# Expert stage of a two-block transformer layer: GpSimd's arithmetic given to VectorE and ScalarE, the gate matrix spread over 72 up tiles, the gather moved later

## The chip, the cores and the metric

One NeuronCore of a Trainium2 chip runs the whole program in one launch. The metric is device time in microseconds. In this text PE is TensorE, DVE is VectorE, ACT is ScalarE, POOL is GpSimd and SP is SyncE, which only issues DMAs here. Each engine works through its own list of instructions in order, so an instruction that waits holds back all that stand behind it on its engine.

## The reference

512 tokens of width 1024 pass two transformer blocks in float32. The first block has stick-breaking attention, a state-space branch, cross-attention and a feed-forward network. The second has window attention, gated linear attention and, at its end, the part that the change touches: a feed-forward network of 16384 product-key experts.

```
q = (h @ wq).reshape(B, S, PEER_HEADS, 2, PEER_QDIM // 2)
sub_scores = jnp.einsum('bshpk,hpnk->bshpn', q, subkeys)
top_v, top_i = lax.top_k(sub_scores, PEER_TOPK)
...
best_v, best_pos = lax.top_k(cand, PEER_TOPK)
gates = jax.nn.softmax(best_v, axis=-1)
...
ub = jnp.take(u, eb, axis=0)
hid = gelu(jnp.einsum('tkd,td->tk', ub, xb)) * gb
return jnp.einsum('tk,tkd->td', hid, jnp.take(v, eb, axis=0))
```

Each token chooses 128 experts (8 heads times 16). An expert has a first and a second key number, both below 128. Its row of `u` gives a hidden value, which is weighted by its gate and multiplied with its row of `v`.

## The kernel before

**Tiling.** The tokens form four tiles of 128. For the first three tiles (384 tokens) the kernel multiplies with all experts on PE and sets the gates of the experts that a token hasn't chosen to zero. The 16384 experts are 128 expert tiles. An "up tile" is u h for one of them: 24 matmuls of 128x384 (L126 to L128: 8 slices of the width, each as three products of high and low parts). A "down tile" adds its part of the output: 18 matmuls of 128x512. The last token tile gathers instead: 128 rows of `u` and 128 rows of `v` for each token, each step one indirect DMA (L1272) of 128 rows, then one DVE instruction, a dot product (L1282) or an accumulation (L74).

**Split of a weight.** A weight tile `ws` of 128x1024 arrives by an SP DMA (L106). ACT writes its high part (L77, `wh` or `hi`), then L118 subtracts it to get the low part (`wl` or `lo`). `lo_pool` sends the subtraction to POOL, otherwise it is DVE's. Before the change POOL subtracts for half of the last 12 query weights (L1142) and for all but the first of the 128 up tiles (L1302, L1411); the down weights are DVE's.

**Gates and gate matrix.** `gates` turns the top-16 lists of a token tile into key numbers and gates (`sel`), nearly all of it on DVE. `matrix` then makes, for each of the 128 tokens of a tile, a 128x128 matrix of gates over (first key, second key): `o1` is the one-hot of the 128 first keys, `o2` the one-hot of the second keys times the gate (L1234, DVE), and their product on PE (L1235; the profile counts two PE instructions for each). The work goes by groups of 4 tokens, 32 groups for a tile, 96 in all. `MIX` says who makes a group's `o1`: DVE in one instruction (D, L1229), POOL in four (P, L1232), or ACT in five (A, L1227 and L1228: four of |key - column|, one of max(0, 1 - that)). ACT copies each group's product to `G` (L1236), and every 8 groups an ACT DMA takes `G` to DRAM (`scr_g`, L1238).

**Three parts of the stage.** In the up part, `NST` up tiles run while `select` makes the gates and the matrix, `SS` steps of it for each tile; their hidden values go to DRAM (`scr_h`). From tile `EA` on, `RA` gather steps follow each tile. In the ring the other 128 - NST expert tiles have their up and down tiles in turn, with `GA` gather steps each. In the down-only part the down tiles of the first NST follow, with `GB` gather steps each, and hidden values and gates are read back. In the up part a planner lays out each engine's list from the order of the code and its own costs; from the ring on the order is that of the code (L1389 and after).

Of the kernel before, what the change touches and what calls it, by code (L numbers as in the profile page):

```python
# [15 lines left out]
OP = mybir.AluOpType  # L16
# [13 lines left out]
class Split:  # L30
    """A float32 tensor as two float32r parts whose sum is exact."""
# [8 lines left out]
class Kern:  # L40
# [14 lines left out]
    def big(self, pool):  # L55
        """Split [128, 8, 512] in a pool that holds one of them."""
        return Split(pool.tile([128, 8, 512], F32R, name="hi"), pool.tile([128, 8, 512], F32R, name="lo"))

    def open_norm(self, ctx, bufs=2):
        """Room for the rows and the scratch of the norms over D."""  # L60
        self.rows = ctx.enter_context(self.tc.tile_pool(name="rows", bufs=bufs, reuse_waits="tile"))

# [22 lines left out]
    def row_dma(self, t, src, n, eng=None):  # L85
        """A row of DRAM to all partitions."""
        (eng or self.nc.gpsimd).dma_start(t, bass.AP(tensor=src.tensor, offset=src.offset, ap=[[0, 128], [1, n]]))
# [6 lines left out]
    def split_to(self, dst, src, scale=None):  # L94
        """dst.hi, dst.lo from a float32 source; the scale is applied in float32 first."""
# [34 lines left out]
    def tmode(self, ps, w, hT, m=128, nk=8, first=True, last=True):  # L130
        """ps[m, tok] += (nk k-tiles of w)^T hT."""
# [3 lines left out]
    def staggered(self, ws, hT):  # L135
        """tmode for each of ws, the first half of the tokens first; the pending tiles of hT come between."""
# [8 lines left out]
    def nmode(self, ps, ws, hT, tt, k0=0, first=True, last=True):  # L145
        """ps[tok tile tt, 512] += hT^T (two k-tiles in each w)."""
# [18 lines left out]
    def transpose_split(self, src, dst, tt, k0=0, nk=8):  # L165
        """src [128 tok, nk*128] -> dst[:, k0 + k, tok tile tt]."""
# [14 lines left out]
    def norm_T(self, x, row, dst, tt, shift=None, keep=None, wait=False):  # L181
        """dst's token tile tt = the normed x, transposed; with wait, its last part comes with flush()."""
# [8 lines left out]
    def post_norm(self, pss, row, x):  # L191
        """x += rms_norm(the two banks) * row."""
# [6 lines left out]
    def log1p(self, pool, e, out, shape, tag):  # L199
        """out = log(1 + e) for 0 <= e <= 1, as 2 artanh(e / (2 + e))."""  # L200
# [14 lines left out]
# ======================================================================  # L215
# stick-breaking attention
# ======================================================================
def stick_breaking(K, hT, oT, wv, fill):
    tc, nc, I = K.tc, K.nc, K.I
    with ExitStack() as st:  # L220
# [22 lines left out]
        def project(hp, nm):  # L243
            """Queries or keys of two heads. For head j, q2[:, j] holds the queries' high parts in its own
            half of the partitions and the low parts in the other, k2[:, j] the keys' high parts in both
            and kl the keys' low parts in its own."""
# [17 lines left out]
        def weights(h):  # L264
            """The weights of head h, by query."""
# [25 lines left out]
        def values(h, rows):  # L291
            """The weighted values of head h, in three steps."""
# [48 lines left out]
# ======================================================================  # L341
# state-space branch
# ======================================================================
def ssd_steps(K, hT, p):
    """dt and its decays: dt, the cumulative sums of a dt, their exponentials and dt times the decay to
    the chunk's end, by token; the sums and the decay over a chunk by head in DRAM."""
# [48 lines left out]
def ssd(K, hT, acc, steps, last, merge):  # L395
    scr, nat, cd = steps
    tc, nc, I = K.tc, K.nc, K.I
    with ExitStack() as st:
# [29 lines left out]
        def front(g):  # L428
            """The projections of group g; a piece of them at each step."""
# [113 lines left out]
# ======================================================================  # L543
# first block
# ======================================================================
def nmode_pairs(K, name, nk, hT, pool, done, loads=lambda dh: None):
    """hT^T W for a W of 1024 columns, token tile by token tile; loads(dh) starts after each half of W."""
# [18 lines left out]
def block1_mix(K, hT):  # L566
    """The merged branches, transposed, in the buffer of hT."""
    tc, nc, I = K.tc, K.nc, K.I
    scr = K.dp.tile([8, 128, 2, 512], F32, name="scr_br")
    with ExitStack() as st:  # L570
# [50 lines left out]
        def last():  # L621
            """Gates of the state-space branch, beside its last group."""
# [25 lines left out]
# ======================================================================  # L648
# cross-attention
# ======================================================================  # L650
# [10 lines left out]
def mem_kv(K, mT, kT, v):  # L661
    """Keys (transposed) and values of the memory."""
# [15 lines left out]
def queries(K, p, hT):  # L678
    """The queries of a head, transposed, at each step."""
# [50 lines left out]
# ======================================================================  # L730
# feed-forward network
# ======================================================================
# [54 lines left out]
# ======================================================================  # L787
# second block
# ======================================================================
# [11 lines left out]
def modulation(K):  # L801
    """silu(c) w_ada + b_ada, as a row in DRAM, the scales as 1 + scale times the norm's weights; a tile of
    w_ada at each step."""
# [37 lines left out]
def gla_gates(K, q, hT, b):  # L841
    """b: per-chunk cumulative sums of log a, transposed."""
# [27 lines left out]
def window_attention(K, q, pq, qT, kT, vT, mixT):  # L870
    """Sliding-window attention, a block of queries in three steps."""
# [52 lines left out]
def gla_scores(K, A, lm, zp, b, gq, gk):  # L924
    """A[c][s, head, t]: the decayed products of keys and queries within a chunk, a level of the
    hierarchy of halves at each step."""
# [40 lines left out]
def gla_out(K, pw, pq, A, b, gq, gk, v, sg, mixT):  # L967
    """The states before the chunks, then the outputs of all chunks, gated by sg. The room is that of the
    attention's tiles."""
# [57 lines left out]
def block2_mix(K, p, hT, gv, mixT):  # L1027
    """Attention over a window and gated linear attention, transposed, in mixT, and the first half of the
    output projection of two token tiles."""
    tc, nc, I = K.tc, K.nc, K.I  # L1030
    with ExitStack() as st:
# [9 lines left out]
        with ExitStack() as sw:  # L1041
# [22 lines left out]
            def gates(tt):  # L1064
                """silu(gg) and the norm's weights."""
# [32 lines left out]
# ======================================================================  # L1098
# product-key experts
# ======================================================================  # L1100
# The tokens of the first three tiles meet all experts on the tensor engine, weighted by a matrix of
# gates that is zero where an expert isn't chosen; those of the last tile gather their experts' rows.
# [3 lines left out]
NST = 56  # L1106
SS = 2.4
GA = 2.4
RA = 1.4
EA = 18  # L1110
MIX = "DPDA"
GB = 0.7
# [4 lines left out]
def top16(K, sc, tv, ti):  # L1117
    """The 16 largest values of sc in descending order, and where they are; sc is overwritten."""
# [8 lines left out]
class Peer:  # L1127
# [3 lines left out]
    def queries(self, p):  # L1131
        """The 16 best keys of each half query of each token."""
# [4 lines left out]
        for f in range(16):  # L1137
            if f < 4:
                ps = first[f]
            else:  # L1140
                ps = K.gsum()
                K.tmode(ps, K.weight(I["w_pq"][f], lo_pool=f % 2 > 0), self.hT)  # L1142
# [10 lines left out]
    def gates(self, w, tt):  # L1153
        """sel: for each token of the tile and each of its 128 choices, both key numbers and the gate. Pair
        (a, b) of the sorted keys has (a + 1)(b + 1) - 1 others before it that are no smaller, so the 16 first
        of all 256 are among (0, b), (a, b < 8) for 0 < a < 8 and (a, 0), kept here in the order of the pairs."""
# [50 lines left out]
    def matrix(self, w, tt, sel):  # L1207
        """The gates of a tile's tokens for all experts, to DRAM."""
# [6 lines left out]
        for tb in range(0, 128, TB):  # L1215
            G = K.pA.tile([128, 128, TB], F32, name="G", tag="lo" if tb // TB % 2 else "hi")
            Gt = G.rearrange("p b t -> p t b")
            for t0 in range(0, TB, 4):
# [9 lines left out]
                elif who == "D":  # L1228
# [413 lines left out]
```

## Time and profile before

| | |
|---|---|
| time before, median of 3 runs | 3011.12 us (3010.54 to 3011.23) |
| span of the profiled execution | 3010.5 us |
| PE busy | 2898.0 us, 96% |
| DVE busy | 2127.6 us, 71% |
| ACT busy | 1219.5 us, 41% |
| POOL busy | 1143.6 us, 38% |
| DMA | 536.17 MB, mean 178 GB/s |

The profiled execution has no time of its own beside its span; the span lies 0.6 us below the median of the runs. A busy share over the whole span says little here, since the parts differ: the rows below are cut by part, at the first up matmul (1739), the first one-hot matmul (1810), the end of the last one (2138), the first down matmul (2167) and the last up matmul (2757).

### The profile page before, as it was taken

The numbers are of one execution on the slowest core, as the hardware profiler recorded it, in microseconds if no ns is written. First come the engines' busy times: TensorE is split into PE (matmuls) and PEld (weight loads), VectorE is DVE, ScalarE is ACT, GpSimd is POOL, SyncE is SP. The second block draws the span as 40 slices with busy tenths as digits, with TensorE's granted clock in tenths as the row PEclk, the third lists the DMA queues.
The fourth block names the chain that finished last, engine by engine and source line by source line (L and its number), as shares of the span: only waits on it lengthen the run. The fifth ranks groups of instructions, "written<-read, shape, count | busy, mean of one in ns | idle before, by whom it ended". The sixth has DMA issues, their size and how long they took to land.

```text
span 3010.5 us, 38769 instructions
## 1 busy us (share of the span) xinstructions
PE 2898.0 (96%) x14347; PEld 2419.2 (80%) x14347; DVE 2127.6 (71%) x3449; ACT 1219.5 (41%) x1914; POOL 1143.6 (38%) x824
## 2 busy tenths in 40 slices
PE   8999999999999999999999988878999999999998
PEld 6666777777798877787768888878899999998886
DVE  4776355776665656545776998988788888887875
ACT  4654244333344333123443346666333333333333
POOL 0221253342210100001221255777788878775310
PEclk9999999999999999999999998999999999999999
DMA  4112423233542466432203244777898888889983
GB/s 166 50 38 65 159 74 112 81 90 127 185 137 94 140 225 197 139 124 81 62 29 121 84 155 149 254 243 254 292 316 297 293 302 297 299 299 318 344 298 132
DMA packets 212937, 536.17 MB, mean 178 GB/s; under 512 B 17518, under 2 KB 97822, under 8 KB 211084
## 3 DMA queue, kind: packets, MB, share of 16 engines
q1 hardware_dynamic: 151040, 346.27, 35.0%
q0 software_dynamic: 38560, 139.05, 13.3%
q10 hardware_dynamic: 23148, 48.37, 4.5%
q8 instruction: 113, 1.85, 0.3%
q14 instruction: 76, 0.62, 0.1%
HBM read 491.07 MB, written 42.56 MB: 177 GB/s over the span
## 4 chain that ended last, share of the span: by engine, by line
PE 42%; DVE 9%; issue 1%; ACT 1%; POOL 0%; POOLq 0%; ACTq 0%
PE pg L127 9%; PE pg L126 9%; PE pg L128 9%; PE pa L128 4%; PE pa L127 4%; PE pa L126 4%; DVE o L1234 3%; PE pa L1235 2%; DVE oh L1194 1%; DVE gr L1282 1%; DVE o L1229 1%; PE pa L935 1%; PE pg L919 0%; DVE bits L1192 0%; PE pa L1147 0%
## 5 line engine op out<-in xcount | busy, mean ns | idle before, releaser
L126 PE MATMUL pg<-hi,wh 128*128 128x512 f32 (+3 forms) x2272 | 830.8, 366 | 0.5 <-ACT hi L77 0.5
L127 PE MATMUL pg<-lo,wh 128*128 128x512 f32 (+3 forms) x2272 | 829.7, 365 | 0.0
L128 PE MATMUL pg<-hi,wl 128*128 128x512 f32 (+3 forms) x2272 | 825.0, 363 | 2.6 <-POOL wl L118 2.6
L77 ACT ACTIVATE wh<-ws 128x1024 fp32r<-128x1024 f32 (+1 forms) x454 | 461.3, 1021 | 535.0 <-PE pg L127 321.6
L118 POOL TENSOR_TENSOR wl<-ws,wh 128x1024 fp32r<-128x1024 f32 (+1 forms) x177 | 465.5, 2635 | 339.3 <-ACT wh L77 291.3
L118 DVE TENSOR_TENSOR wl<-ws,wh 128x1024 fp32r<-128x1024 f32 (+1 forms) x277 | 331.8, 1205 | 213.6 <-ACT wh L77 213.0
L126 PEld LDWEIGHTS pg<-hi,wh 128*128 128x128 f32 (+1 forms) x2272 | 430.2, 190 | 54.9 <-issue 4.0
L127 PEld LDWEIGHTS pg<-lo,wh 128*128 128x128 f32 (+1 forms) x2272 | 431.0, 190 | 53.5 <-issue 3.5
L128 PEld LDWEIGHTS pg<-hi,wl 128*128 128x128 f32 (+1 forms) x2272 | 430.3, 189 | 52.9 <-POOL wl L118 3.0
L161 POOL TENSOR_SCALAR ss<-ss 128x1 f32<-128x1 f32 x54 | 15.3, 283 | 621.0 <-ACT junk L77 620.0
L1272 POOL DMA_INDIRECT gr<-in_peer_v,idx x128 | 198.4, 1550 | 123.3 <-DVE acc L74 99.1
L74 DVE SCALAR_TENSOR_TENSOR acc<-gr,hid,acc 128x1024 f32<-128x1024 f32 x127 | 234.7, 1848 | 9.1 <-DMA gr<-in_peer_v,idx 7.2
L1282 DVE SCALAR_TENSOR_TENSOR gr<-gr,h 128x1024 f32<-128x1024 f32 x128 | 225.5, 1791 | 12.7 <-DMA gr<-in_u_rows,idx 12.5
L1272 POOL DMA_INDIRECT gr<-in_u_rows,idx x128 | 189.6, 1481 | 78.7 <-DVE gr L1282 47.0
L77 ACT ACTIVATE hid<-pg 128x384 f32<-128x384 f32 x128 | 62.6, 489 | 303.8 <-PE pg L128 303.6
L126 PE MATMUL pg<-wh,hi 128*128 128x512 f32 x448 | 181.8, 407 | 2.0 <-ACT hi L77 2.0
L1234 DVE TENSOR_SCALAR o<-io,sT 128x128 f32<-128x128 f32 x384 | 164.6, 500 | 26.6 <-PE pa L1235 26.6
L128 PE MATMUL pg<-wh,lo 128*128 128x512 f32 x448 | 179.9, 402 | 3.3 <-DVE lo L98 1.7
L127 PE MATMUL pg<-wl,hi 128*128 128x512 f32 x448 | 179.8, 401 | 3.2 <-POOL wl L118 2.0
L77 ACT ACTIVATE ah<-hid 128x384 fp32r<-128x384 f32 x128 | 67.2, 525 | 260.0 <-DVE hid L68 255.7
L1235 PE MATMUL pa<-o,o 128*128 128x128 f32 x768 | 110.2, 291 | 55.8 <-DVE o L1234 52.0
L1235 PEld LDWEIGHTS pa<-o,o 128*128 128x128 f32 x768 | 102.2, 199 | 62.9 <-issue 28.3
(426 smaller groups left out, 5197.0 us busy)
## 6 DMA issues: line engine op xcount, KB each, us to landing
ws<-in_peer_u SPq DMA_DIRECT2D x128, 512.0 KB
ws<-in_peer_v SPq DMA_DIRECT2D x128, 512.0 KB
ws<-in_w_ada SPq DMA_DIRECT2D x48, 512.0 KB
scr_g<-G ACTq DMA_DIRECT2D x12, 2048.0 KB
gt<-scr_g SPq DMA_DIRECT2D x32, 768.0 KB
ws<-in_w_xbc SPq DMA_DIRECT2D x24, 512.0 KB
ws<-in_w_gate SPq DMA_DIRECT2D x22, 512.0 KB
ws<-in_w_up SPq DMA_DIRECT2D x22, 512.0 KB
```

The lines of the kernel that those rows point to most:

```text
L74: return self.nc.vector.scalar_tensor_tensor(out, a, s, b, op0=op0, op1=op1)
L77: return self.nc.scalar.activation(out, in_, f, **k)
L118: eng.tensor_tensor(w.lo, s, w.hi.bitcast(F32), op=OP.subtract)
L126: mm(ps, a.hi, b.hi, start=first, stop=False)
L127: mm(ps, a.hi, b.lo, start=False, stop=False)
L128: mm(ps, a.lo, b.hi, start=False, stop=last)
L935: nc.tensor.matmul(ps[:, i, :], l[hp, i, ls], r[hp, i, rs], start=True, stop=True)
L1194: nc.vector.copy_predicated(T[:, :, :, :n], bits[:, :, :, None].to_broadcast([128, 8, TOPK, n]), src)
L1234: self.o2_last = nc.vector.tensor_scalar(o2[:, t, :], self.io, sT[:, 1, c:c + 1], sT[:, 2, c:c + 1], op0=OP.is_equal, op1=OP.mult)
L1235: nc.tensor.matmul(pg_[:, t, :], o1[:, t, :], o2[:, t, :], start=True, stop=True)
L1272: nc.gpsimd.indirect_dma_start(out=r, out_offset=None, in_=table, in_offset=bass.IndirectOffsetOnAxis(ap=self.idx[:, z, k:k + 1], axis=0))
L1282: nc.vector.scalar_tensor_tensor(rows[k], rows[k], 1.0, self.h3, op0=OP.mult, op1=OP.mult, accum_out=self.dot[:, k:k + 1])
```

## The change

POOL keeps no arithmetic in the expert stage: `lo_pool` falls away for the query weights and the up tiles, so their subtractions go to DVE, and `MIX` has no P group. Of four groups three now have their `o1` from ACT and one from DVE, where it was one and two. `NST` rises from 56 to 72, with fewer steps of gates and matrix for each tile (`SS` 1.8, was 2.4). The gather takes 0.8 steps for each late up tile (was 1.4), 3.0 for each ring tile (was 2.4) and 0.6 for each down-only tile (was 0.7). Docstrings and comments are dropped as well, which moves line numbers by 3 (L1234, L1272 and L1282 become L1231, L1269 and L1279).

```
-NST = 56
-SS = 2.4
-GA = 2.4
-RA = 1.4
+NST = 72
+SS = 1.8
+GA = 3.0
+RA = 0.8
 EA = 18
-MIX = "DPDA"
-GB = 0.7
+MIX = "AADA"
+GB = 0.6
...
-                K.tmode(ps, K.weight(I["w_pq"][f], lo_pool=f % 2 > 0), self.hT)
+                K.tmode(ps, K.weight(I["w_pq"][f]), self.hT)
...
-                elif who == "D":
+                else:
                     nc.vector.tensor_tensor(o1, self.io[:, None, :].to_broadcast([128, 4, 128]), ...
-                else:
-                    for t, c in enumerate(cs):
-                        nc.gpsimd.tensor_scalar(o1[:, t, :], self.io, sT[:, 0, c:c + 1], None, op0=OP.is_equal)
...
-        w = w or K.weight(K.I["peer_u"][e], lo_pool=e > 0)
+        w = w or K.weight(K.I["peer_u"][e])
...
-                        us[jobs[i]] = K.wsplit(us[jobs[i]], lo_pool=True)
+                        us[jobs[i]] = K.wsplit(us[jobs[i]])
```

The first place is DVE's list where the gates of the last token tile are worked out, before any one-hot (`pos`, `bits`, `oh`, `sel` are scratch of the gates). Before:

```order
L1175 TENSOR_SCALAR pos<-bp 128x128
L1176 TENSOR_SCALAR pos<-bp 128x128
L74 SCALAR_TENSOR_TENSOR pos<-pos 128x128
L1178 TENSOR_SCALAR pos<-pos 128x128
L1179 TENSOR_SCALAR pos<-pos 128x128
L71 ISA pos<-pos 128x256 x2
L65 TENSOR_TENSOR pos<-pos 128x128
L1192 TENSOR_SCALAR bits<-pos 128x128 x2
L1194 COPY_PREDICATED oh<-bits,tif 128x1024
L1194 COPY_PREDICATED oh<-bits,oh 128x128x4
```

Now:

```order
L118 TENSOR_TENSOR wl<-ws,wh 128x1024
L1175 TENSOR_SCALAR pos<-bp 128x128
L1176 TENSOR_SCALAR pos<-bp 128x128
L118 TENSOR_TENSOR wl<-ws,wh 128x1024
L74 SCALAR_TENSOR_TENSOR pos<-pos 128x128
L1178 TENSOR_SCALAR pos<-pos 128x128
L65 TENSOR_TENSOR sel<-bv 128x128
L1179 TENSOR_SCALAR pos<-pos 128x128
L71 ISA pos<-pos 128x256 x2
L65 TENSOR_TENSOR pos<-pos 128x128
L1192 TENSOR_SCALAR bits<-pos 128x128 x2
L1194 COPY_PREDICATED oh<-bits,tif 128x1024
```

The subtractions of the up tiles now stand between the steps of the gates. Up to DVE's first one-hot its list holds 245 subtractions of L118 from the program's start, where it held 219; ten of the 26 more stand before the last key search (L1120), sixteen after it. On PE, 375 up matmuls stand before the first one-hot matmul (279 before), and 72 after the last one up to the ring's two first up tiles (96 before).

The second place is ACT's list in the matrix part. Before:

```order
L77 ACTIVATE G<-pa 128x4x128 x2
L77 ACTIVATE o_15543<-io,sT 128x128 x4
L77 ACTIVATE wh<-ws 128x1024
L77 ACTIVATE o_15543<-o_15543 128x512
L77 ACTIVATE hid<-pg 128x384
L77 ACTIVATE wh<-ws 128x1024
L77 ACTIVATE G<-pa 128x4x128
L77 ACTIVATE oh<-tif 128x1024
```

Now:

```order
L77 ACTIVATE o_15574<-o_15574 128x512
L77 ACTIVATE G<-pa 128x4x128
L77 ACTIVATE o_15628<-io,sT 128x128 x4
L77 ACTIVATE o_15645<-io,sT 128x128
L77 ACTIVATE o_15628<-o_15628 128x512
L77 ACTIVATE o_15645<-io,sT 128x128 x3
L77 ACTIVATE wh<-ws 128x1024
L77 ACTIVATE hid<-pg 128x384
L77 ACTIVATE G<-pa 128x4x128
L77 ACTIVATE o_15645<-o_15645 128x512
```

Two one-hot groups of ACT (`o_15628`, `o_15645`) now stand around one weight's high part and one hidden tile, where one group stood around two.

The third place is DVE's list in the ring. Before:

```order
L118 TENSOR_TENSOR lo<-ws,hi 128x1024
L68 TENSOR_TENSOR hid<-hid,gt 128x384
L98 TENSOR_TENSOR al<-hid,ah 128x384
L1282 SCALAR_TENSOR_TENSOR gr,dot<-gr,h_12392 128x1024 x2
L118 TENSOR_TENSOR lo<-ws,hi 128x1024
```

Now:

```order
L118 TENSOR_TENSOR lo<-ws,hi 128x1024
L68 TENSOR_TENSOR hid<-hid,gt 128x384
L98 TENSOR_TENSOR al<-hid,ah 128x384
L118 TENSOR_TENSOR wl<-ws,wh 128x1024
L1279 SCALAR_TENSOR_TENSOR gr,dot<-gr,h_12392 128x1024 x3
```

Each cycle has the subtraction of the next up tile and always three gather steps, where it had two or three. POOL's list from the key search on is 256 indirect DMAs without anything between, and the norms' small instructions after them.

## Rows read from the trace of the kernel before

**Rows 1.** Stages, busy us (x): PE, PEld, DVE, ACT, POOL; clock, DMA share, GB/s
```profile
1640.00:1739.00 99.00, 97.74 (x546) 82.43 (x545) 77.48 (x476) 32.94 (x47) 21.46 (x9) 1.00 0.26 79
1739.00:1810.00 71.00, 57.85 (x317) 56.77 (x315) 65.79 (x323) 36.09 (x49) 39.81 (x22) 0.93 0.52 168
1810.00:2138.00 328.00, 278.76 (x1724) 272.17 (x1725) 291.30 (x639) 202.27 (x310) 231.62 (x177) 0.94 0.67 227
2138.00:2167.00 29.00, 26.37 (x142) 25.97 (x141) 15.77 (x17) 6.05 (x11) 17.99 (x11) 0.94 0.98 347
2167.00:2757.00 590.00, 590.00 (x2943) 533.26 (x2943) 495.61 (x455) 204.22 (x282) 476.45 (x241) 1.00 0.88 301
...
2800.00:2900.00 100.00, 100.00 (x431) 80.98 (x430) 78.67 (x96) 38.66 (x52) 33.12 (x19) 1.00 0.98 340
```

**Rows 2.** Waits of PE, 1747 to 2162: total us, times, longest us
```profile
PE pa L1235 <- DVE o L1234: 52.0, 22, 6.6
```

**Rows 3.** Timeline of DVE: start us, us, operation, count, idle before
```profile
1962.41 8.54 DVE L1234 TENSOR_SCALAR o<-io,sT 128x128 f32<-128x128 f32 x4
...
1985.21 1.11 DVE L1234 TENSOR_SCALAR o<-io,sT 128x128 f32<-128x128 f32 x4 [0.46 <-PE pa L1235]
```

**Rows 4.** Timeline of POOL, same stretch
```profile
1963.38 6.96 POOL L118 TENSOR_TENSOR wl<-ws,wh 128x1024 fp32r<-128x1024 f32 x3
```

**Rows 5.** Timeline of PE: first one-hots, an unhindered run, a ring cycle
```profile
1809.92 2.04 PE L1235 MATMUL pa<-o,o 128*128 128x128 f32 x8 [6.58 <-DVE o L1234]
...
1978.17 1.95 PE L1235 MATMUL pa<-o,o 128*128 128x128 f32 x16
...
2306.15 0.34 PE L126 MATMUL pg<-hi,wh 128*128 128x384 f32 x1
...
2310.39 0.39 PE L126 MATMUL pa<-hi,ah 128*128 128x512 f32 x1
...
2314.57 0.34 PE L126 MATMUL pg<-hi,wh 128*128 128x384 f32 x1
```

**Rows 6.** Timeline of ACT in the matrix part
```profile
1987.04 1.25 ACT L77 ACTIVATE o<-io,sT 128x128 f32<-128x128 f32 x4
1988.18 1.06 ACT L77 ACTIVATE wh<-ws 128x1024 fp32r<-128x1024 f32 x1
1989.13 0.63 ACT L77 ACTIVATE o<-o 128x512 f32<-128x512 f32 x1
1990.29 0.49 ACT L77 ACTIVATE hid<-pg 128x384 f32<-128x384 f32 x1 [0.53 <-PE pg L128]
...
1992.05 1.93 ACT L77 ACTIVATE G<-pa 128x512 f32<-128x512 f32 x2 [0.33 <-PE pa L1235]
```

**Rows 7.** Timeline of DVE among the gates of tile 3
```profile
1758.44 0.36 DVE L1192 TENSOR_SCALAR bits<-pos 128x128 uint32<-128x128 uint32 x2
...
1760.75 2.57 DVE L1192 TENSOR_SCALAR bits<-pos 128x128 uint32<-128x128 uint32 x2
```

**Rows 8.** Timeline of DVE, one ring cycle
```profile
2303.68 1.21 DVE L118 TENSOR_TENSOR lo<-ws,hi 128x1024 fp32r<-128x1024 f32 x1
2304.82 0.55 DVE L68 TENSOR_TENSOR hid<-hid,gt 128x384 f32<-128x384 f32 x1
2306.01 0.58 DVE L98 TENSOR_TENSOR al<-hid,ah 128x384 fp32r<-128x384 f32 x1 [0.65 <-ACT ah L77]
2306.52 1.21 DVE L1282 SCALAR_TENSOR_TENSOR gr<-gr,h 128x1024 f32<-128x1024 f32 x1
...
2307.77 3.29 DVE L1282 SCALAR_TENSOR_TENSOR gr<-gr,h 128x1024 f32<-128x1024 f32 x1
```

**Rows 9.** Timeline of POOL, the same cycle
```profile
2306.01 0.94 POOL L1272 DMA_INDIRECT gr<-in_u_rows,idx  x1 [0.30 <-issue]
2307.01 2.97 POOL L118 TENSOR_TENSOR wl<-ws,wh 128x1024 fp32r<-128x1024 f32 x1
```

**Rows 10.** Timeline of DVE, down-only part
```profile
2848.24 1.23 DVE L118 TENSOR_TENSOR wl<-ws,wh 128x1024 fp32r<-128x1024 f32 x1 [0.39 <-ACT wh L77]
```

## The prediction

> **What bounds the kernel now.** I cut the span by the parts of the expert stage first [rows 1], since the whole-span shares mix parts with different limits. The reader is to see three things there. In the ring, from 2167, PE is busy for the whole 590 us at clock 1.00. In the up part it isn't: 57.9 of 71, 278.8 of 328 and 26.4 of 29 us, at a granted clock of 0.93 to 0.94, between the two levels of 1.2 and 2.4 GHz. And DVE is the fullest of the engines that feed PE there: 291.3 of 328 us, 89%.
>
> Then the cost of PE's work where nothing hinders it [rows 5]: 24 up matmuls take 4.24 us (2306.15 to 2310.39), 18 down matmuls 4.18, one-hot matmuls 1.95 / 16 = 0.122 us each. So the up part needs 56 x 4.24 + 768 x 0.122 = 237.4 + 93.7 = 331 us of PE, plus 8.5 for the ring's two first up tiles. It takes 428 (1739 to 2167): some 88 us are lost, which is more than PE's idle time, because PE also runs slower around its waits.
>
> Then who PE waits for: of the waits by name the longest are for the one-hots of L1234, 52.0 us in 22 waits [rows 2]. Last, why DVE is late: four one-hots take 1.11 us, but the four that start at 1962.41 take 8.54 [rows 3], and they end when three POOL subtractions, 1963.38 to 1970.34, do [rows 4]. So while POOL subtracts, such a DVE instruction stands still. The ring has the same with a dot product: 1.21 us, and 3.29 beside a POOL subtraction [rows 8, 9]. There it costs nothing, since PE is the bound.
>
> **The change part by part.** The parts follow each other on PE, so I go by where each ends.
>
> *Beginning, 1739 to the first one-hot.* PE now has 375 up matmuls there: 375 / 24 x 4.24 = 66.3 us, so by PE the first one-hot could come at 1805, 5 us earlier than 1809.9 [rows 5]. By DVE it comes later: 26 more subtractions stand before it, at 1.14 us (2303.68 to 2304.82, [rows 8]) 29.6 us. Against this the gates of the first two tiles lose their blocked instructions. The trace has four of the kind in [rows 7], 2.57 us where the same pair takes 0.36: 4 x 2.2 = 8.8 us back. That bounds it at 20.8 us later. Ten of the 26 stand among the key searches, where DVE is busy 77.5 of 99 us [rows 1], so they have room: I take them at nothing, and the other 16 at 18.2 - 8.8 = 9.4. Value +10, bounds -5 and +21.
>
> *Matrix, from first to last one-hot, 328 us now.* It held 40.4 up tiles (56 less 11.6 before it and 4 behind it) and holds 53.4. PE needs 53.4 x 4.24 + 93.7 = 320. ACT becomes the fullest feeder [rows 6]. Per tile it has a high part (0.95, 1988.18 to 1989.13) and a hidden tile (0.49); per group a copy of the product (1.93 / 2 = 0.97); per group of its own 1.14 + 0.63 = 1.77. Before: 40.4 x 1.44 + 96 x 0.97 + 24 x 1.77 = 194; its 202.3 busy us [rows 1] leave 8.6 for the rest. After: 76.9 + 92.6 + 127.4 + 8.6 = 306. DVE has 384 one-hots (1.11 for four: 107), 53 subtractions (60) and 43 dots (0.8 for each tile from 18 to 71; 52), 219 together. The 24 groups of its own and the gates of two tiles come on top, and it stays below ACT unless these take over 87 us.
>
> No row shows ACT this full, so I bound by the nearest rows. Lower end: PE's 320. Upper end: the loss of before stays, 328 - 265 = 63, with another cause: 383. If the fullest feeder is again busy 89% of the time, it is 306 / 0.888 = 344. I take 335, between that and PE's floor, since what held DVE were blocks of several us, and ACT has none. Value 335 - 328 = +7, bounds -8 and +55.
>
> *End of the up part.* Behind the last one-hot stand 3 up tiles instead of 4: -4.2. They cover the last gates' way to DRAM and back. A tile less of cover may cost up to those 4.2 us: I take +2, bounds 0 and 4.
>
> *Ring and down-only part.* 16 up tiles have left the ring; the 128 down tiles all remain: -16 x 4.24 = -67.8. This holds if PE stays the bound. DVE's new cycle is 1.14 (v) + 1.19 (gate to `al`) + 0.51 + 1.14 (u) + 3 x 1.21 [rows 8] + 0.39 of waiting for the high part [rows 10] = 8.00 of PE's 8.42 us: it fits, with 0.42 to spare. DMA moves 301 GB/s now [rows 1]. 0.6 more gathers of 128x1024 float32 in 8.42 us add 37: 338 GB/s. The highest that the rows show over a stage are 340 and 347, at a share of 0.98. So it just fits: I take +3 for late gathers, bounds 0 and +58 (were 301 the ceiling, 8.42 x 338 / 301 = 9.46 us a cycle, 56 times).
>
> *Nothing elsewhere.* The gather now ends behind the last tile, 2 accumulations and 2 operations of 1.21 us on DVE. The last three down tiles, 54 matmuls of 4.18 / 18, lie beside them on PE (12.5 us). Without that cover it would be 4.8 us.
>
> Sum: 10 + 7 - 4.2 + 2 - 67.8 + 3 = -50. From the span of 3010.5 that is 2960.5, and the median of the runs lies 0.6 higher: 2961 us.
>
> **The rivals.**
>
> *A, ACT takes DVE's place.* ACT works in order, and its list has copies and hidden tiles that wait for PE between one-hots that PE waits for. If PE gets no more out of the matrix than now, 265 / 328 = 0.81, and ACT likewise, it takes 306 / 0.81 = 378: +43 on the forecast, 3004. For it: ACT at 96% of PE's floor. Against it: ACT is idle for 126 of the 328 us now, and its high parts have five buffers (the pool `w`) and can run ahead of PE.
>
> *B, DMA bounds the ring.* If the mix of gathers and weights yields 320 GB/s, a cycle takes 8.42 x 338 / 320 = 8.89, +26 over 56 cycles, 2984. For it: the share of 0.88 at 301 GB/s would be 0.99. Against it: 347 in the stage from 2138 to 2167 [rows 1].
>
> *C, the gathers block DVE as the subtractions did (slower).* Place: the ring, three gathers a cycle, each an instruction on POOL of 0.94 us [rows 9]. Price: 3 x 0.94 less the 0.42 to spare, 2.4 us for 56 cycles, +134 on the forecast: 3095. It decides from (50 + 56 x 0.42) / 168 = 0.44 us per gather on. Against it: the dot of 2306.52 runs its plain 1.21 us and starts inside the gather that POOL has from 2306.01 to 2306.95 [rows 8, 9]. The Trainium skill (SBUF — State Buffer, Who interferes with whom) says that a VectorE instruction with two SBUF inputs contends with a GpSimd one that reads SBUF, for the whole instruction; a gather reads its row numbers there, and by this rule C's 3095 would be the time. The row of the dot disagrees, so C stays small.
>
> *D, all feeders come in time.* First one-hot at 1805, matrix 320, nothing for gates and gathers: 2961 - 15 - 15 - 2 - 3 = 2926. Against it: ACT at 96% of that floor, in order.
>
> **How the numbers follow.** Forecast 0.60, A 0.14, B 0.12, C 0.04, D 0.10. The range reaches from near D, 2930, to near A, 3000, and leaves out C, half of A and some of D. A measurement here can tell 0.2%, 6 us, from no change. Faster: the forecast, B and D and nearly half of A, 0.87. Same: the rest of A, 0.07. Slower: C and the ends of A and B, 0.06.
>
> **What would show it.** The first one-hot matmul comes at about 1820 and the last 335 us later. Four one-hots on DVE take 1.1 to 1.4 us throughout; a block of several us would prove the cause wrong. PE's waits in the matrix name ACT's one-hots, not L1234. The ring has PE at 100%, 8.42 us a cycle, dots of 1.21 us, DMA near 338 GB/s. The prediction is wrong if the matrix takes over 360 us, if a ring cycle is longer than 8.5, or if dots stretch beside gathers.

## The result

The changed kernel takes 2960.09 us (median of 4 runs, 2959.05 to 2961.24), the kernel before 3011.18 us beside it. The ratio is 0.9831, 95% interval 0.9817 to 0.9845: 51 us, 1.7% faster. The forecast was 2961.

The profiled execution has a span of 2958.7 us, against 3010.5. Cut by what PE does, as in the prediction, the difference of 51.8 us falls on the parts like this (us; the ring and the down-only part are taken together, up to the span's end):

| part | before | after | difference |
|---|---|---|---|
| up to the first up matmul | 1739.4 | 1744.3 | +4.9 |
| beginning, to the first one-hot matmul | 70.5 | 75.1 | +4.6 |
| gate matrix, to the end of the last one-hot | 327.7 | 336.9 | +9.2 |
| to the first down matmul | 29.4 | 24.3 | -5.1 |
| ring, down-only part and end | 843.5 | 778.1 | -65.4 |

So the time is won where PE was already at its bound (the ring has 16 up tiles fewer), because the part that took these tiles over hardly grew: the matrix part got 12.5 tiles more (1247 up matmuls for 946), 53 us of PE's time, in 9 us.

### The profile page after: what moved, and what is told of

Read it like the earlier page. It is cut to its first block, busy times and chain, and to the rows that moved or that the text cites. A ratio compares the mean times of both kernels' runs of the same rounds, so it can differ in the third digit from the quotient of the medians.

```text
span 2958.7 us, 38765 instructions
## 1 busy us (share of the span) xinstructions
PE 2880.6 (97%) x14347; PEld 2400.9 (81%) x14347; DVE 2038.0 (69%) x3558; ACT 1293.3 (44%) x2154; POOL 667.7 (23%) x595
## 5 line engine op out<-in xcount | busy, mean ns | idle before, releaser
L77 ACT ACTIVATE wh<-ws 128x1024 fp32r<-128x1024 f32 (+1 forms) x470 | 479.0, 1024 | 553.2 <-PE pg L127 311.7
L118 DVE TENSOR_TENSOR wl<-ws,wh 128x1024 fp32r<-128x1024 f32 (+1 forms) x426 | 513.2, 1211 | 274.0 <-ACT wh L77 273.4
L1269 POOL DMA_INDIRECT gr<-in_u_rows,idx x128 | 169.2, 1322 | 588.6 <-DVE gr L1279 371.4
L1269 POOL DMA_INDIRECT gr<-in_peer_v,idx x128 | 188.7, 1475 | 326.0 <-DVE acc L74 298.3
L74 DVE SCALAR_TENSOR_TENSOR acc<-gr,hid,acc 128x1024 f32<-128x1024 f32 x127 | 162.7, 1281 | 2.0
L1279 DVE SCALAR_TENSOR_TENSOR gr<-gr,h 128x1024 f32<-128x1024 f32 x128 | 151.9, 1218 | 4.1 <-DMA gr<-in_u_rows,idx 4.1
L1231 DVE TENSOR_SCALAR o<-io,sT 128x128 f32<-128x128 f32 x384 | 106.7, 349 | 61.7 <-PE pa L1232 55.5
L118 POOL TENSOR_TENSOR wl<-ws,wh 128x1024 fp32r<-128x1024 f32 (+1 forms) x44 | 101.2, 2304 | 141.7 <-ACT wh L77 131.3
L98 DVE TENSOR_TENSOR al<-hid,ah 128x384 fp32r<-128x384 f32 x128 | 71.6, 560 | 79.1 <-ACT ah L77 79.1
L127 PE MATMUL pa<-wl,ah 128*128 128x512 f32 x288 | 114.5, 397 | 0.0
```

The costliest lines, as they stand in the source:

```text
L74: return self.nc.vector.scalar_tensor_tensor(out, a, s, b, op0=op0, op1=op1)
L77: return self.nc.scalar.activation(out, in_, f, **k)
L98: return self.nc.vector.tensor_tensor(dst.lo, src, dst.hi.bitcast(F32), op=OP.subtract)
L118: eng.tensor_tensor(w.lo, s, w.hi.bitcast(F32), op=OP.subtract)
L127: mm(ps, a.hi, b.lo, start=False, stop=False)
L1231: self.o2_last = nc.vector.tensor_scalar(o2[:, t, :], self.io, sT[:, 1, c:c + 1], sT[:, 2, c:c + 1], op0=OP.is_equal, op1=OP.mult)
```

## The profile after

The stages first, cut at the events of the table and at the first matmul of the down-only part. The columns are those of [rows 1]: length, busy time (instructions) of PE, PEld, DVE, ACT and POOL, then granted clock, DMA share and GB/s.

```profile
1640.00:1744.30 104.30, 99.98 (x548) 84.26 (x548) 88.52 (x489) 32.92 (x48) 0.00 (x0) 0.98 0.24 76
1744.30:1819.40 75.10, 72.44 (x421) 71.93 (x420) 73.08 (x336) 43.35 (x65) 5.69 (x5) 1.00 0.57 182
1819.40:2156.30 336.90, 316.48 (x2023) 307.44 (x2024) 245.54 (x651) 289.22 (x566) 50.19 (x40) 0.99 0.68 240
2156.30:2180.60 24.30, 21.18 (x121) 20.86 (x119) 11.33 (x17) 6.00 (x10) 8.44 (x6) 1.00 1.00 378
2180.60:2646.00 465.40, 465.40 (x2304) 419.59 (x2305) 390.05 (x472) 162.01 (x223) 221.22 (x165) 1.00 0.94 336
```

In the third row the order of the feeders has changed: ACT is busy for 289 us of 337 and DVE for 246, where DVE had 291 and ACT 202 of 328 [rows 1]. PE's granted clock there is 0.99, where it was 0.94. In the ring PE is busy the whole time, as before, and DMA moves 336 GB/s instead of 301.

Whom PE waits for by name, from 1739 to 2210 (total us, times, longest), where [rows 2] had 52.0 us for L1234:

```profile
PE pa L1232 <- ACT o L77: 9.9, 18, 1.3
PE pg L128 <- DVE wl L118: 9.7, 4, 6.9
PE pa L126 <- ACT ah L77: 3.1, 1, 3.1
PE pa L1232 <- DVE o L1231: 2.7, 1, 2.7
PE pg L126 <- ACT wh L77: 0.6, 1, 0.6
```

DVE's one-hots are no longer there but for the first. (L1234 is L1231 now, and L1235 is L1232.) The low parts in the second line are a price of the change itself. In the longest of these four waits the high part is there at 1900.62, but DVE is in the middle of the gates' key searches (L1120 to L1124), which follow each other in its list from 1899.67 to 1907.12 without a break, and the subtraction stands behind them:

```profile
1899.57 1.05 ACT L77 ACTIVATE wh<-ws 128x1024 fp32r<-128x1024 f32 x1
```
```profile
1907.82 1.22 DVE L118 TENSOR_TENSOR wl<-ws,wh 128x1024 fp32r<-128x1024 f32 x1
```
```profile
1909.09 0.69 PE L128 MATMUL pg<-hi,wl 128*128 128x384 f32 x1 [6.95 <-DVE wl L118]
```

In two more of the four the subtraction also starts 3.3 us after its high part is there, with DVE busy until then; only the shortest wait, 0.6 us, follows straight upon ACT.

Shortest, median and longest of the 384 one-hots that DVE makes on that line, in ns, first of before and then of after:

```profile
L1234 DVE TENSOR_SCALAR o<-io,sT x384: 278/337/7770, 1809.4 to 2134.9; 128x128 f32<-128x128 f32 x192
```
```profile
L1231 DVE TENSOR_SCALAR o<-io,sT x384: 287/341/580, 1818.9 to 2152.7; 128x128 f32<-128x128 f32 x192
```

The median is the same; the tail of up to 7.77 us is gone. It was the tail that PE waited for.

The matmul rows of PE: the first one-hots, a run of 16 with its successor, and the starts of the ring's up and down groups.

```profile
1819.41 1.17 PE L1232 MATMUL pa<-o,o 128*128 128x128 f32 x8 [2.67 <-DVE o L1231]
...
1983.72 1.95 PE L1232 MATMUL pa<-o,o 128*128 128x128 f32 x16
1985.42 0.42 PE L126 MATMUL pg<-hi,wh 128*128 128x384 f32 x1
...
2304.43 0.34 PE L126 MATMUL pg<-hi,wh 128*128 128x384 f32 x1
...
2308.68 0.39 PE L126 MATMUL pa<-hi,ah 128*128 128x512 f32 x1
...
2312.87 0.34 PE L126 MATMUL pg<-hi,wh 128*128 128x384 f32 x1
```

A ring cycle is 8.44 us (2304.43 to 2312.87); it was 8.42 in [rows 5]. The second and third lines show a price that the prediction had too high: 16 one-hot matmuls take 1.70 us from start to start, 0.106 each. The 1.95 of the row contains the end of the last one, which overlaps with what follows.

With that price and the counts of the windows, PE's own work in the matrix part is 1247 up matmuls of 4.24 / 24 = 0.177 and 768 one-hots of 0.106: 220 + 82 = 302 us after, and 946 x 0.177 + 82 = 249 before. What the part takes beyond that is called its loss below: 79 us before, 35 after. For the other kernels it is reckoned with the same 302 us at 72 tiles and 249 at 56; their own counts of up matmuls (1239 to 1258, and 939 to 946) would move it by less than 2 us.

And DVE beside POOL's gathers in the ring, one cycle of each:

```profile
2306.35 1.22 DVE L1279 SCALAR_TENSOR_TENSOR gr<-gr,h 128x1024 f32<-128x1024 f32 x1
...
2307.49 1.22 DVE L1279 SCALAR_TENSOR_TENSOR gr<-gr,h 128x1024 f32<-128x1024 f32 x1
```
```profile
2307.84 1.68 POOL L1269 DMA_INDIRECT gr<-in_u_rows,idx  x1 [3.90 <-DVE gr L1279]
```

The dot products take 1.22 us whether a gather runs beside them or not: of the 128 in the whole run, 61 overlap a gather, and the longest of these takes 1.23. The one of 3.29 us in [rows 8] has no counterpart.

## The experiments

The question was which of the two halves of the change earns the 51 us: the work taken from POOL, or the spread of the gate matrix over 72 tiles instead of 56. And what is still lost in the matrix part. The parts of all kernels, cut as above (us; the time is the median of the timed runs, the ratio is to the kernel before):

| kernel | first up at | beginning | matrix | its loss | to first down | ring and down | time | ratio [95%] |
|---|---|---|---|---|---|---|---|---|
| before | 1739.4 | 70.5 | 327.7 | 79 | 29.4 | 843.5 | 3011.18 | 1 |
| after | 1744.3 | 75.1 | 336.9 | 35 | 24.3 | 778.1 | 2960.09 | 0.9831 [0.9817, 0.9845] |
| e1 POOL free, old spread | 1746.0 | 63.5 | 333.8 | 85 | 27.2 | 844.4 | 3013.42 | 1.0005 [0.9995, 1.0015] |
| e2 new spread, POOL as before | 1738.2 | 78.9 | 353.5 | 51 | 21.7 | 808.1 | 2997.37 | 0.9953 [0.9937, 0.9969] |
| e3 after, half the query splits on POOL | 1737.7 | 75.1 | 337.1 | 35 | 24.4 | 777.3 | 2953.37 | 0.9811 [0.9796, 0.9827] |
| e4 after, mix ADDA | 1741.9 | 75.0 | 315.7 | 14 | 22.9 | 778.3 | 2934.37 | 0.9748 [0.9733, 0.9764] |
| e5 as e1, mix ADDA | 1742.6 | 65.4 | 296.8 | 48 | 26.1 | 839.0 | 2976.95 | 0.9892 [0.9876, 0.9907] |
| e6 after, ring's splits on POOL | 1744.3 | 75.2 | 337.5 | 35 | 24.2 | 803.1 | 2985.87 | 0.9916 [0.9901, 0.9931] |
| e7 after, e3 and e4 together | 1737.1 | 75.9 | 315.6 | 14 | 21.2 | 770.9 | 2930.82 | 0.9735 [0.9722, 0.9748] |
| e8 as e4, up splits on POOL | 1742.5 | 80.4 | 352.6 | 51 | 22.7 | 776.7 | 2978.72 | 0.9897 [0.9882, 0.9912] |
| e9 after, old pace of the gather | 1743.8 | 75.2 | 340.1 | 38 | 28.2 | 778.3 | 2962.24 | 0.9830 [0.9811, 0.9849] |

Parts are compared rather than spans, since the profiled executions of e5, e6 and e7 had down-only matmuls of 388 to 394 ns where the others have 397; the span of e7 (2920.7) lies 10 us below its median.

### e1_pool_free: the work taken from POOL, at the old spread

The changed code with the table of before, except for the mix of the one-hots:

```diff
-NST = 72
-SS = 1.8
-GA = 3.0
-RA = 0.8
+NST = 56
+SS = 2.4
+GA = 2.4
+RA = 1.4
...
-GB = 0.6
+GB = 0.7
```

> GpSimd without arithmetic, but the old spread and gather (56 up tiles, SS 2.4, GA 2.4, RA 1.4, GB 0.7). Theory (GpSimd's subtractions held DVE, and DVE held PE): a good part of the gain is here already. But 40 up tiles in the matrix need only 265 us of PE, while ACT with three groups of four has 40.4 x 1.44 + 92.6 + 127.4 + 8.6 = 287, so now ACT is the bound: matrix 290 to 320 us instead of 328, total 2975 to 3003. PE's waits name ACT, no DVE one-hot is blocked for microseconds. Rival (the gain is the spread over more up tiles): 3005 to 3017, no change.

Measured: ratio 1.0005, no difference. The theory's number was missed, and the rival's was hit. The matrix part's row and PE's waits by name:

```profile
1809.50:2143.30 333.80, 281.93 (x1717) 268.24 (x1716) 244.82 (x703) 271.09 (x540) 57.27 (x48) 0.92 0.63 222
```
```profile
PE pa L1232 <- ACT o L77: 36.4, 36, 4.9
PE pa L1232 <- DVE o L1231: 8.1, 3, 6.6
PE pa L1212 <- ACT sel L77: 6.8, 1, 6.8
```

DVE's blocks are gone here as well (its longest one-hot is 0.55 us), but the wait has got another name: ACT, busy for 271 us where PE's own work is 249. The one-hots that left POOL and DVE made ACT fuller than PE, and the loss is 85 us, as large as before. So this run shows what the freed POOL is worth with the mix AADA; e5 has another mix.

### e2_spread_only: the new spread, with POOL's work kept

The code of before, mix DPDA included, with the other numbers of the change:

```diff
-NST = 56
-SS = 2.4
-GA = 2.4
-RA = 1.4
+NST = 72
+SS = 1.8
+GA = 3.0
+RA = 0.8
...
-GB = 0.7
+GB = 0.6
```

> The new spread and gather (72 up tiles, SS 1.8, GA 3.0, RA 0.8, GB 0.6), but GpSimd keeps its subtractions and one group of four, MIX as before. Theory: DVE's one-hots are still blocked for microseconds, PE still waits for them by name, and in the ring one dot of each cycle stretches by 2.1 us, so DVE needs about 1.14 + 1.19 + 0.51 + 3 x 1.21 + 2.1 = 8.6 of PE's 8.42 us and the ring becomes DVE's by up to 10 us: total 2990 to 3020. Rival (the spread gives the gain): 2961 to 2975.

Measured: 0.9953, some 14 us, within the theory's range. The loss in the matrix part is 51 us, and the ring, which takes 465 us in the changed kernel, takes 495, three times the "up to 10 us" more that the theory had for it:

```profile
1817.10:2170.60 353.50, 327.15 (x2034) 320.02 (x2035) 309.17 (x623) 219.84 (x336) 247.69 (x188) 0.97 0.68 232
...
2192.30:2687.70 495.40, 481.27 (x2304) 412.94 (x2305) 415.82 (x419) 155.80 (x223) 402.89 (x221) 1.00 0.91 317
```

So neither half earns the 51 us: alone they are worth 0 and 14. Two questions followed. Is it ACT's load that made e1 fail (e4, e5)? And what stretched e2's ring (e6)?

### e3_queries_on_pool: half of the queries' subtractions back on POOL

```diff
-                K.tmode(ps, K.weight(I["w_pq"][f]), self.hT)
+                K.tmode(ps, K.weight(I["w_pq"][f], lo_pool=f % 2 > 0), self.hT)
```

> The changed kernel, but half of the query weights have their subtraction on GpSimd again (6 of them). The changed kernel starts its first up matmul at 1744.3 instead of 1739.4. If the subtractions that stand among the key searches on DVE cause this, it comes back: first up matmul 1740, total 2955 to 2957. Rival (DVE's later start of the gates decides, wherever PE starts): 2959 to 2961, since the 6 subtractions saved on DVE lie in its idle time.

Measured: 2953.37, 6.7 us below the changed kernel. The intervals of the two ratios overlap, so the times alone don't settle it. In the trace the first up matmul comes 6.6 us earlier (1737.7 against 1744.3), and every later part has the same length within 1 us. But 1.9 of the 6.6 lie ahead of the edit: the first matmul of the key scores (L1147) is at 1655.1 against 1657.0. From there to the first up matmul it is 82.6 us here, 87.3 in the changed kernel. The other kernels agree: 82.6 in the three more that keep these subtractions on POOL (before, e2, e7), 85.8 to 88.3 in the six more that don't. So the edit is worth some 4.7 us, and the six subtractions cause it, as the theory said; that the total lies below its 2955 to 2957 is owed to the earlier start. Its query part beside the first row of after:

```profile
1640.00:1737.70 97.70, 96.44 (x536) 81.25 (x535) 80.52 (x480) 32.92 (x47) 14.35 (x6) 1.00 0.25 82
```

DVE is busy for 8 us less there; PE waits 1.0 us for the copied queries, where the changed kernel waits 4.1.

### e4_mix_half: half of the one-hot groups on DVE

```diff
-MIX = "AADA"
+MIX = "ADDA"
```

> The changed kernel with MIX ADDA: ACT makes the one-hots of two groups of four instead of three, DVE of two instead of one. If ACT's load (306 of 337 us) is what is left of PE's waits in the matrix, 42 us less of it bring the matrix from 337 towards PE's 320: 325 to 330, total 2948 to 2954. Rival (DVE is as near to the bound, the 24 more groups cost it 14 us): matrix 337 or longer, total 2960 to 2968.

Measured: 2934.37, 25.7 us below the changed kernel: the direction of the theory, at over twice the size it gave. Of the 24.9 us between the two spans, 21.2 lie in the matrix part.

```profile
1816.90:2132.60 315.70, 310.41 (x2014) 306.73 (x2015) 263.61 (x680) 251.95 (x449) 46.69 (x41) 0.99 0.73 260
```
```profile
PE pa L1232 <- DVE o L1231: 3.6, 3, 1.9
PE pa L1232 <- ACT o L77: 2.8, 6, 1.0
PE pa L126 <- ACT ah L77: 1.7, 1, 1.7
```

ACT falls by 37 us and DVE rises by 18. Now both stay well below PE's 302, and the loss is 14 us. PE's waits for ACT's one-hots fall from 9.9 to 2.8 us. The waits for the low parts (9.7 us) are gone as well, and they were not ACT's: the planner lays out every list anew when `MIX` changes, and the longest unbroken run of key searches on DVE is 3.8 us here, where it was 7.45. So the gain has two causes, less load on ACT and a better order on DVE, and this run can't tell their shares apart. The expectation was too small because it still counted PE's work as 320 us, and it knew only the first of the two.

### e5_old_spread_mix: the same mix at the old spread

e1 with one line changed:

```diff
-MIX = "AADA"
+MIX = "ADDA"
```

> The earlier run without GpSimd arithmetic at the old spread (56 up tiles in the gate part, mix AADA), now with mix ADDA. Part with the gate matrix there: 333.8 us, PE's own work 946 x 0.177 + 768 x 0.107 = 249 us, ScalarE busy 271. Theory (ScalarE, fuller than PE, was the bound there): 24 groups leave it at 1.57 each (289.2 to 252.0 between the changed kernel and its ADDA form), so ScalarE falls to 234 and VectorE rises to 263; the part falls to 275 to 300 us and the whole to 2953 to 2982 us. Rival (too few up tiles stand between the one-hots, whoever makes them; only the spread helps): the part stays above 320 and the time above 3000 us.

Measured: 2976.95, 36 us below e1; the theory's range, not the rival's.

```profile
1808.00:2104.80 296.80, 265.36 (x1719) 254.51 (x1718) 257.57 (x727) 235.38 (x428) 61.72 (x47) 0.98 0.71 251
```

The matrix part's row has ACT at 235 us, and the part falls from 333.8 to 296.8. So ACT's load, or the order that goes with it, was e1's bound, and not the number of tiles beside the one-hots. But the loss remains 48. DVE at 258 now stands above PE's 249, yet PE's longest waits by name are still for ACT's one-hots, which leaves open how the two share this loss:

```profile
PE pa L1232 <- ACT o L77: 23.3, 20, 7.3
```

At 72 tiles the same mix loses 14. That is, by the loads, what the spread does: the feeders' load from the one-hots is the same, each added tile gives PE 4.24 us of work and the feeders about 1.4 (ACT) and 1.1 (DVE), so PE becomes the fullest of the three.

### e6_ring_pool: the ring's subtractions back on POOL

```diff
-                        us[jobs[i]] = K.wsplit(us[jobs[i]])
+                        us[jobs[i]] = K.wsplit(us[jobs[i]], lo_pool=True)
```

> The changed kernel, with the subtraction of the ring's up weights (56 of them) back on GpSimd; all else as changed. Theory (a GpSimd subtraction holds up one dot product a cycle, from 1.21 to about 3.2 us, and with three gathers a cycle VectorE no longer fits): 8.00 - 1.14 + 2.0 = 8.9 us a cycle against PE's 8.42, and the spread-alone run had 495.4 us in this part against 465.4; so + 25 to + 32 us, 2985 to 2993 us. Rival (that part was long in the spread-alone run for another reason, such as DMA; GpSimd's subtraction only takes VectorE's place): within 5 us of the changed kernel, 2955 to 2965 us.

Measured: 2985.87, 25.8 us slower than the changed kernel, as the theory said. Only the ring changes, to 494.2 us from 465.4. Its row, and one cycle of DVE and POOL:

```profile
2181.20:2675.40 494.20, 479.27 (x2296) 411.26 (x2297) 414.21 (x416) 154.45 (x221) 402.80 (x220) 1.00 0.90 314
```
```profile
2300.50 2.96 DVE L1279 SCALAR_TENSOR_TENSOR gr<-gr,h 128x1024 f32<-128x1024 f32 x1 [0.37 <-DMA gr<-in_u_rows,idx]
...
2304.68 1.23 DVE L1279 SCALAR_TENSOR_TENSOR gr<-gr,h 128x1024 f32<-128x1024 f32 x1 [1.21 <-DMA gr<-in_u_rows,idx]
```
```profile
2299.39 2.99 POOL L118 TENSOR_TENSOR wl<-ws,wh 128x1024 fp32r<-128x1024 f32 x1
2302.77 1.53 POOL L1269 DMA_INDIRECT gr<-in_u_rows,idx  x1 [0.39 <-issue]
```

The dot that is issued at 2300.50, while POOL subtracts until 2302.38, ends at 2303.46: it stood still and then ran its 1.1 us. The gather behind the subtraction starts late too (2302.77), and dots now wait for their rows, as the one at 2304.68 does: 23.5 us in 28 waits over the ring, where the changed kernel has one of 0.9. Behind the dots stand DVE's next product with the gates and, after it, ACT's split of the gated tile (`ah`), for which PE waits. The changed kernel has no such wait in its ring. DVE's waits and PE's in e6's ring:

```profile
DVE gr L1279 <- DMA gr<-in_u_rows,idx: 23.5, 28, 1.7
```
```profile
PE pa L126 <- ACT ah L77: 17.6, 24, 3.2
```

Three gathers a cycle and the subtraction don't fit together. That is the second way in which the halves need each other: the new spread leaves 56 ring cycles instead of 72 for the gather, hence 3 a cycle.

### e7_mix_and_queries: the two gains together

The changed kernel with the edits of e3 and e4.

> The changed kernel with mix ADDA and half of the queries' subtractions back on GpSimd. Theory (the two act in different parts, one in the query part, one in the gate matrix): the sum of both gains less what the ADDA run already had in the query part (first up matmul 2.4 us earlier): 2934.4 - 4 = 2930, from 2926 to 2932 us. Rival (they share the room in VectorE's queue, so that one gain swallows the other): 2933 to 2938 us.

Measured: 2930.82, ratio 0.9735 (0.9722 to 0.9748): the sum, within the theory's range. It is the fastest of the kernels run, 29 us below the change. Its interval overlaps with that of e4, so that the 3.5 us between these two are not settled by the times; the first up matmul is at 1737.1 against 1741.9, with the same start of the query part within 0.2 us.

### e8_up_pool: the cause put back by itself

e4 with the subtractions of the gate part's up tiles on POOL, as before the change:

```diff
-        w = w or K.weight(K.I["peer_u"][e])
+        w = w or K.weight(K.I["peer_u"][e], lo_pool=e > 0)
```

> The changed kernel with mix ADDA, and the subtractions of the 72 up tiles in the gate part back on GpSimd. Against the ADDA run (2934.4 us, gate matrix part 315.7). Theory (GpSimd's subtractions block VectorE's one-hots for several us, whatever its load): one-hots of up to 7 us are back, PE waits for them by name, the part takes 335 to 365 us, the time is 2953 to 2985 us. Rival (only VectorE's load counts; 52 subtractions of 1.14 us, 59 us, leave it): the part stays at 310 to 318 and the time at 2929 to 2937 us.

Measured: 2978.72, 44 us slower than e4. The theory's range was hit. DVE lost 59 us of its own work, and yet the matrix part grew by 36.9 us:

```profile
1822.90:2175.50 352.60, 324.44 (x2016) 316.23 (x2016) 305.72 (x621) 254.64 (x450) 172.71 (x92) 0.97 0.67 230
```
```profile
L1231 DVE TENSOR_SCALAR o<-io,sT x384: 315/339/7766, 1818.6 to 2171.4; 128x128 f32<-128x128 f32 x192
```
```profile
PE pa L1232 <- DVE o L1231: 25.7, 20, 4.4
```

DVE executes fewer instructions (621 for 680) and is busy for longer (305.7 for 263.6). The tail of 7.77 us is back. Beside each other:

```profile
1959.03 3.16 DVE L1231 TENSOR_SCALAR o<-io,sT 128x128 f32<-128x128 f32 x4
...
1971.04 2.55 DVE L1192 TENSOR_SCALAR bits<-pos 128x128 uint32<-128x128 uint32 x2
```
```profile
1958.40 2.94 POOL L118 TENSOR_TENSOR wl<-ws,wh 128x1024 fp32r<-128x1024 f32 x1 [1.31 <-ACT wh L77]
...
1971.00 2.51 POOL L118 TENSOR_TENSOR wl<-ws,wh 128x1024 fp32r<-128x1024 f32 x1 [0.17 <-ACT wh L77]
```

Both DVE groups end when POOL's subtraction does, or up to a plain duration later. The Trainium skill (SBUF — State Buffer, Who interferes with whom) describes this as a lock on a shared port that one instruction holds to its end; for subtractions the trace agrees. A one-hot can also stay behind several subtractions in a row: the longest of the four in [rows 3], 7.77 us, starts at 1962.67 and ends 0.1 us behind the third of [rows 4].

POOL's other work, the one-hots of the P groups, went with the change too, and no run put it back alone. But the trace of before acquits it. There 119 of DVE's 384 one-hots ran beside POOL's one-hots and nothing else of POOL, and the longest of these took 0.47 us; each of the 15 over 0.8 us ends 0.08 to 0.11 us behind the end of a subtraction. So do the 27 over 0.8 us in e8 (0.08 to 0.10). A P group and eight of DVE's one-hots beside it, before:

```profile
1947.10 3.58 POOL L1232 TENSOR_SCALAR o<-io,sT 128x128 f32<-128x128 f32 x4
```
```profile
1946.77 2.40 DVE L1234 TENSOR_SCALAR o<-io,sT 128x128 f32<-128x128 f32 x8
```

### e9_gather_early: the gather's old pace in the changed kernel

```diff
-GA = 3.0
-RA = 0.8
+GA = 2.4
+RA = 1.4
...
-GB = 0.6
+GB = 0.7
```

> The changed kernel (mix AADA), with the gather's old pace: 1.4 rows' steps for each up tile from the 18th on instead of 0.8 (75 against 43 before the ring), 2.4 a cycle in the ring instead of 3. 32 more dot products of 1.21 us, 39 us, stand in VectorE's list in the gate matrix part (245.5 us busy of 336.9 there). Theory (the feeders' load counts there, and VectorE's instructions stand between one-hots in order): VectorE comes to 284, near ScalarE's 289; the part grows by 5 to 20 us to 342 to 357, the ring does not gain (PE busy 100% there), so 2965 to 2980 us. Rival (ScalarE alone bounds that part and VectorE has 91 us to spare): no difference, 2956 to 2964 us.

Measured: 2962.24, ratio 0.9830 against 0.9831: no difference, as the rival said. In the profiled execution the matrix part is 3 us longer and the way to the first down matmul 4 us, in which PE waits 7.1 us for the gated tile instead of 3.1. DVE's 32 additional dots cost next to nothing: it had the room.

```profile
PE pa L126 <- ACT ah L77: 7.1, 1, 7.1
```

So doing the gather later is not a gain of its own that these runs can tell from zero.

## Why the prediction was right

**The cause.** That POOL's subtractions hold up DVE's one-hots, and PE behind them, is shown by e8: the subtractions alone bring back the tail, the wait by name and 37 us. What the prediction did not say is that taking them away gains nothing at the old spread with the mix of the change (e1). It treated the spread as a way to move tiles, and the blocks as the loss; in fact the load of the feeders, ACT's above all, would have kept the loss at 85 us, had PE not been given more work in the same part. With the mix ADDA the old spread does gain, 36 us over e1 (e5).

**First one-hot, +10.** It came 9.5 us later (1819.4), but by other terms. The ten early subtractions that were costed at nothing delay the first up matmul by 4.9 us. The six of the query weights among them are enough for that: e3 puts them back on POOL, and some 4.7 us return. Then the count of up matmuls before the first one-hot, 375 (279 before), was too small. The trace has 409, and 302 before. PE's groups between 1744.3 and 1819.4 after the change (count | busy us, mean ns | idle us before them):

```profile
L126 PE MATMUL pg<-hi,wh 128*128 128x384 f32 x137 | 46.1, 336 | 0.0
L128 PE MATMUL pg<-hi,wl 128*128 128x384 f32 x136 | 45.6, 335 | 0.0
L127 PE MATMUL pg<-lo,wh 128*128 128x384 f32 x136 | 45.6, 335 | 0.0
```

At 0.177 each these are 72.3 of the beginning's 75.1 us. So PE itself sets the first one-hot, and DVE, to which the step gave 9.4 us, costs only the wait of 2.67. Two errors cancelled.

**Matrix, +7.** It grew by 9.2 us, to 336.9, where 335 was forecast. That ACT becomes the feeder that matters was right (e4, e5); its load was 289 us rather than 306. PE's floor was wrong: 302 us, not 320, with 52 tiles instead of 53.4 and one-hots at 0.106 instead of 0.122, which had been read from a row's duration instead of from start to start. With the measured loads the same step would have gone from a floor of 302 to 289 / 0.888 = 326, and its value, taken at the same place between the two, would have been 317. So that the value came out is luck: two loads that were 17 and 18 us too high made up for 20 us that the step didn't have. One wait it had at nothing: the subtractions were counted as load on DVE (53, 60 us), but not their place in its list behind the gates, which makes 9 of the 20 us that PE waits by name in this part. Rival D, all feeders in time, was therefore priced 18 us too dear: e4 is 4 us below its 320.

**End of the up part, -2.2.** Measured -5.1. The shorter cover costs the 3.1 us of PE's wait for the gated tile, as said (2 us, at most 4.2). Against this, a wait for one of POOL's subtractions went that the prediction had not seen:

```profile
PE pg L128 <- POOL wl L118: 2.6, 1, 2.6
```

The rest, 1.4 us, goes with the granted clock, which is 1.00 here after 0.94 in [rows 1]: before, it fell to 0.80 in the 5 us from 2160.

**Ring and down, -64.8.** Measured -65.4. PE stayed the bound at 8.44 us a cycle. DVE is busy 390 of 465 us, so that its work fits, as forecast. The 3 us for late gathers agree with the result (67.8 - 65.4 = 2.4) by luck: DVE waits for gathered rows once, for 0.9 us, and PE waits for nothing in the ring. Most of the 2.4 us is the first cycle, which takes 10.02 us (2180.59 to 2190.61) where before it took 8.66. It follows PE's wait of 3.1 us for the gated tile, and PE's granted clock is 0.50 there, the lower of its two levels:

```profile
2181.00:2183.00 2.00, 2.00 (x6) 1.52 (x6) 0.96 (x2) 1.93 (x3) 0.00 (x0) 0.50 0.75 307
```

So the shorter cover costs 1.4 us more than the wait itself. The 53 cycles behind it, 8.43 to 8.44 us instead of 8.42, make up some 0.7 us.

**The rivals.** A: its wait did appear by name, but at 10 us instead of 43; in e1, where ACT is above PE, it decides. B: DMA moves 336 GB/s, and the cycle isn't longer. C: dots beside gathers take 1.22 us; the rule that was weighed for C holds for POOL's subtractions and not for these gathers. What e6 adds is that C's place was right and its agent wrong: with the subtraction back on POOL, and no more gathers than in the changed kernel, a cycle takes 8.8 us.

## What to carry to other kernels

Price each part by the fullest engine in it, after the change, and by starts rather than durations: an engine that is blocked by another looks like the bound, and freeing it only pays if what takes over its work is still below the engine to be kept busy. Where feeders are too full in one part and the bound engine has work in another part, moving that work beside the feeders can be worth more than either edit, and the last balance (which of two engines makes a quarter of the one-hots) was here worth half of the whole change again, part of it by a better order. Where a planner lays out the lists, an edit of one constant moves instructions on every engine, so the list of the waiting engine's feeder is to be read before a gain is put down to load. An instruction moved off a shared resource should be tried by putting it back alone (e8), since the changed kernel itself cannot tell its parts apart.

## What was not expected of the hardware

- A DVE instruction with one tensor and constants is held up by POOL's subtraction like one with two tensors: two of L1192 take 2.55 us beside it in e8, and 0.39 us otherwise.
- POOL's gathers, which it executes for 0.93 to 1.99 us in the changed kernel, hold up no dot product (1.23 us at most); behind a subtraction it is the gather that comes late. One thing stays open: 11 of the 27 held one-hots of e8 start 0.3 to 0.7 us before the profile shows the subtraction, while the gather ahead of it is still shown, though the 66 one-hots beside a gather alone took at most 0.55 us.
- PE's wait ahead of the ring cost more than itself: after its 3.1 us the granted clock was 0.50 from 2181 to 2183, and the first cycle took 1.6 us longer than the later ones.
- The down-only matmuls took 397 ns in most profiled executions and 388 to 394 ns in three, at a granted clock of 1.00 in both. What sets this stays open; e7's ring and down-only part, one of the three, is 7 us shorter than that of the changed kernel, and nothing is concluded from that difference.
